# Expert scores and MLP up with one 512-wide matmul over both feature parts, and a search among 136 sums

## Chip, cores and metric

The kernel runs on one core of one Trainium2 chip. The metric is the device time of one execution in microseconds (us); each kernel is run several times and its median counts. PE is the matrix engine (TensorE), DVE is VectorE, ACT is ScalarE, POOL is GpSimd.

## What is computed

Two layers of a transformer with 256 tokens of width 1024 (a retention mixer in the first, a gated spatial unit in the second, each followed by a layer of experts), then a block with convolution and attention, attention to a memory, and an MLP with squared ReLU. All is float32. The change lies in the expert layer, and in the upward product of the MLP:

```python
def peer_ffn(h, w_query, sub_keys, expert_u, expert_v):   # 8 heads, 16 best, 128 keys
    q = (ht @ w_query).reshape(T, Hh, 2, PEER_HALF)
    scores = jnp.einsum('thpd,hpkd->thpk', q, sub_keys)
    s_top, i_top = lax.top_k(scores, K)
    cand = (s_top[:, :, 0, :, None] + s_top[:, :, 1, None, :]).reshape(T, Hh, K * K)
    best, pos = lax.top_k(cand, K)
    expert_idx = jnp.take_along_axis(cand_idx, pos, axis=-1)
    gates = jax.nn.softmax(best, axis=-1)
    a = jax.nn.gelu(jnp.einsum('tkd,td->tk', expert_u[expert_idx], x)) * gates
    return jnp.einsum('tk,tkd->td', a, expert_v[expert_idx])

def squared_relu_mlp(h, w_up, w_down):
    a = jax.nn.relu(h @ w_up)
    return (a * a) @ w_down
```

## The kernel before

**Products.** A float32 product is made of three matmuls in a reduced form of float32: features and weights are each kept as a high part and a low remainder, and high by high, high by low and low by high are added in PSUM (`mm3`, L338 to L342; `f1`, L344, for 128 outputs and 256 tokens: 8 blocks of the feature axis, 24 matmuls of 256 columns). A weight unit is 128x1024. It comes from HBM into `raw`; ACT copies out the high part (L293) and DVE, or POOL for units marked so, subtracts it to get the low part (L295). `pump` (L265) keeps three units split ahead of PE (five from the second half of layer 1's expert scores on), and it is called by `get` (L309) for each unit.

**Experts.** `peer` (L927) does not gather: it scores all 16384 experts, 128 units of 128. `u_units` makes the first 64 units (S1, called here "first half") and later the other 64 (S2): two units share a PSUM tile `pu` of 128x512, and ACT's gelu (L974) takes it to SBUF. Beside S1 runs the search for each token's experts, one small task or two at each unit (`tick`, L177): the 16 best of 128 scores for 16 key halves and two blocks of tokens (`top`, L1138 to L1145, five DVE instructions that search, find and replace), then `routing_rest` (L1147): for each of 8 heads all 256 sums (L1166), their 16 best (`pick`, again `top`), and with them the indices and gates (`prep`, `eq`, `mul`, `tree`). In S1 each fourth weight split goes to POOL. S2 runs beside the `gating` work; after it comes V, the product with the expert values (L1002 to L1106), with 512-wide matmuls.

**MLP up.** For n = 0, 2, ... 30 (L1855): two units into a `pu` tile, Relu on ACT (L1863), the square on DVE (L1865), its split by ACT (L393) and DVE (L394).

**PSUM and order.** The PSUM tiles are one bank of 512 columns each: two with the tag `mm`, two with `st`, four with `acc`. `accs` (L388) lays eight accumulators of 256 columns into the four `acc` tiles; `out_proj` (L505) uses them for the output projections of retention, the gated unit and the memory, and in the last pass a DVE operation adds each finished accumulator to the residual (`put`, L527 and L1820) while PE goes on to the next. V (L1002), the pair of query units and MLP down use `acc` tiles too. The order on each engine is written by hand: it is the order in which the code issues the instructions. A wait is set between instructions of different engines that touch the same tile.

Of the kernel before, what the change touches and what calls it, by code (L numbers as in the profile page):

```python
# [22 lines left out]
P = 128  # L23
# [134 lines left out]
class Net:  # L158
    def __init__(self, ctx, nc, tc, a, out):
        self.ctx, self.nc, self.tc, self.a, self.out = ctx, nc, tc, a, out  # L160
        self.tasks = deque()
        self.timed = {}
        self.later = deque()
        self.clock = 0

# [34 lines left out]
    def plan(self):  # L200
# [152 lines left out]

    def f1_pair(self, pss, tag, hs, shared=False, lag=0):
# [8 lines left out]
    def f2(self, pss, hs, tag, after=None, qs=range(4)):  # L363
        mm = self.nc.tensor.matmul
        for q in qs:
            s = self.get(tag)
            w = s.rearrange("p s (c m) -> p s c m", c=2)
            for tb in range(2):
                tt = slice(tb * P, tb * P + P)
                for c in range(2):  # L370
                    hi, lo = hs[2 * q + c]
# [13 lines left out]
    def acc_tile(self, name):  # L385
        return self.p_ps.tile([P, 512], F32, tag="acc", name=name, bufs=4)
# [9 lines left out]
    def split_scaled(self, his, srcs, gs):  # L396
        for (hi, lo), src, g in zip(his, srcs, gs):
            self.nc.scalar.activation(hi, src, AF.Copy, scale=g)  # L398
        for (hi, lo), src, g in zip(his, srcs, gs):
# [147 lines left out]
    def run(self):  # L547
# [9 lines left out]
        self.iota = c.tile([P, TOPK], F32, name="iota")  # L557
# [369 lines left out]
    def peer(self, l):  # L927
# [38 lines left out]
        def u_units(S, done_by, before_last=None, extra=()):  # L966
            for i in range(64):
                if i % 2 == 0:
                    pt = self.mm_tile("pu").rearrange("p (j t) -> p j t", j=2)
# [177 lines left out]
    def routing_rest(self, pr):  # L1147
        nc = self.nc
        H = 8
        sh = [P, H, TOPK, TOPK]  # L1150
        add = self.tasks.append

        def block(tb):
# [5 lines left out]
            def cand(k):  # L1159
                if k == 0:  # L1160
                    r["cand"] = pr.tile(sh, F32, tag="cand", name="cand", bufs=2)
                    r["best"] = pr.tile([P, H, TOPK], F32, tag="best", name="best")
                    r["pos"] = pr.tile([P, H, TOPK], U32, tag="pos", name="pos")
                hh = slice(4 * k, 4 * k + 4)
                s4 = [P, 4, TOPK, TOPK]
                nc.vector.tensor_tensor(r["cand"][:, hh], v4[:, hh, 0, :, None].to_broadcast(s4),  # L1166
                                        v4[:, hh, 1, None, :].to_broadcast(s4), op=ALU.add)

            def pick(h):
                self.top(pr, r["cand"][:, h].rearrange("p a b -> p (a b)"), r["best"][:, h], r["pos"][:, h], T)  # L1170

            def prep():
# [3 lines left out]
                ab = pr.tile([P, 2, H, TOPK], U32, tag="ab", name="ab")  # L1176
                nc.vector.tensor_scalar(ab[:, 0], r["pos"], 4, None, op0=ALU.logical_shift_right)
                nc.vector.tensor_scalar(ab[:, 1], r["pos"], 15, None, op0=ALU.bitwise_and)
                r["abf"] = pr.tile([P, 2, H, TOPK], F32, tag="abf", name="abf")
                nc.vector.tensor_copy(r["abf"], ab)  # L1180
# [644 lines left out]
    def mlp(self):  # L1825
# [29 lines left out]
        for n in range(0, 32, 2):  # L1855
            pt = self.mm_tile("pu").rearrange("p (j t) -> p j t", j=2)
            if n == 0:
                self.f1_pair([pt[:, 0], pt[:, 1]], "mlp_u", hs, True)
            for j in range(2 if n else 0):
                self.f1(pt[:, j], self.get("mlp_u"), hs)  # L1860
            self.tick()
            t = pa.tile([P, 2, T], F32, tag="t", name="t", bufs=2)
            nc.scalar.activation(t, pt, AF.Relu)  # L1863
# [54 lines left out]
```

## Time and profile before

| what | us |
|---|---|
| median of 3 runs | 2551.14 (2549.85 to 6877.75) |
| the profiled execution | 2548.39 |
| its span | 2546.6 |
| PE busy in it | 2483.5 |
| DVE busy | 1906.6 |
| ACT busy | 1257.2 |
| POOL busy | 212.8 |

The granted clock of PE was 0.992 of full speed over the span. The time of a run is that of the whole execution; the span is what the profiler recorded from the first instruction to the last. Busy times overlap, since the engines work beside one another. Times on a timeline are counted from the start of the span.

### The profile page before, as it was taken

Reading aid. Unit: us, or ns where it says so; the run is one execution under the profiler, and the core shown is the slowest. Engines: PE = TensorE matmul, PEld = TensorE weight load, DVE = VectorE, ACT = ScalarE, POOL = GpSimd, SP = SyncE. Lnnn points to the kernel's source line nnn. Section 1 sums busy time; section 2 is a strip of 40 time slices with the busy share of each in tenths; the row PEclk is TensorE's granted clock in tenths of the full one; section 3 lists DMA queues with packets and bytes.
Section 4 is the critical chain, followed back from the end, with each engine's and each line's share of the span. In section 5 each row is a group of like instructions: output and inputs, shape, how many; then the busy total and the mean of one; then the engine's idle time right before and its main releaser. Section 6 shows DMA issues by size and latency. Waiting matters only on the chain.

```text
span 2546.6 us, 43250 instructions
## 1 busy us (share of the span) xinstructions
PE 2483.5 (98%) x17066; PEld 2279.3 (90%) x17066; DVE 1906.6 (75%) x3230; ACT 1257.2 (49%) x1788; POOL 212.8 (8%) x155
## 2 busy tenths in 40 slices
PE   8999999999999999999999999999999999889998
PEld 7979999999988888788999999999888888889986
DVE  7767788888868777865877888888675555785654
ACT  4345544444444455556555444444445444665643
POOL 0000122200000000001122222000000000101000
PEclk8999999999999999999999999999999999999999
DMA  8785545555568888866665455555785655444553
GB/s 311 233 286 188 180 162 190 178 188 189 185 223 293 292 314 298 293 214 214 201 228 169 166 183 185 185 186 195 240 276 196 220 191 178 144 142 158 175 190 124
DMA packets 145195, 532.44 MB, mean 209 GB/s; under 512 B 16208, under 2 KB 16464, under 8 KB 144096
## 3 DMA queue, kind: packets, MB, share of 16 engines
q1 hardware_dynamic: 131616, 477.82, 56.1%
q0 software_dynamic: 12656, 49.62, 5.7%
q8 instruction: 134, 2.20, 0.4%
q10 hardware_dynamic: 720, 2.24, 0.2%
q14 instruction: 69, 0.57, 0.1%
HBM read 507.46 MB, written 22.16 MB: 208 GB/s over the span
## 4 chain that ended last, share of the span: by engine, by line
PE 74%; DVE 10%; DMA 9%; ACT 5%; issue 2%; POOL 0%; ACTq 0%; DVEq 0%; SPq 0%
PE pu L340 11%; PE pu L342 11%; PE pu L341 11%; PE V L1008 6%; PE V L1009 6%; PE V L1007 6%; DVE split L295 5%; DMA raw<-in_pv 4%; ACT split L293 3%; PE g L1275 2%; PE pq L341 1%; PE pq L342 1%; PE pq L340 1%; PE po L341 1%; PE po L342 1%
## 5 line engine op out<-in xcount | busy, mean ns | idle before, releaser
L295 DVE TENSOR_TENSOR split<-raw,split 128x1024 fp32r<-128x1024 f32 x756 | 935.6, 1241 | 515.0 <-ACT split L293 513.7
L293 ACT ACTIVATE split<-raw 128x1024 fp32r<-128x1024 f32 x808 | 851.3, 1057 | 679.2 <-PE V L1009 197.8
L340 PE MATMUL pu<-h,split 128*128 128x256 f32 x2496 | 719.8, 288 | 0.1
L342 PE MATMUL pu<-h,split 128*128 128x256 f32 x2496 | 707.1, 283 | 6.9 <-DVE split L295 6.4
L341 PE MATMUL pu<-h,split 128*128 128x256 f32 x2496 | 706.7, 283 | 0.5 <-DVE h L400 0.5
L342 PEld LDWEIGHTS pu<-h,split 128*128 128x128 f32 x2496 | 478.5, 192 | 8.4 <-DVE split L295 7.6
L341 PEld LDWEIGHTS pu<-h,split 128*128 128x128 f32 x2496 | 478.9, 192 | 0.7 <-DVE h L400 0.7
L340 PEld LDWEIGHTS pu<-h,split 128*128 128x128 f32 x2496 | 478.5, 192 | 0.6 <-ACT u L1436 0.3
L1008 PE MATMUL V<-split,a_sp 128*128 128x512 f32 x1024 | 401.9, 392 | 6.2 <-DVE split L295 6.2
L1007 PE MATMUL V<-split,a_sp 128*128 128x512 f32 x1024 | 402.3, 393 | 0.0
L1009 PE MATMUL V<-split,a_sp 128*128 128x512 f32 x1024 | 401.8, 392 | 0.0
L1008 PEld LDWEIGHTS V<-split,a_sp 128*128 128x128 f32 x1024 | 193.0, 189 | 49.5 <-DVE split L295 7.7
L1009 PEld LDWEIGHTS V<-split,a_sp 128*128 128x128 f32 x1024 | 193.0, 188 | 42.6
L1007 PEld LDWEIGHTS V<-split,a_sp 128*128 128x128 f32 x1024 | 193.1, 189 | 41.7 <-ACT split L293 0.3
L974 ACT ACTIVATE S<-pu 128x512 f32<-128x512 f32 x128 | 76.5, 598 | 232.6 <-PE pu L342 232.6
L295 POOL TENSOR_TENSOR split<-raw,split 128x1024 fp32r<-128x1024 f32 x52 | 134.0, 2576 | 527.2 <-ACT split L293 527.2
L300 DVE SCALAR_TENSOR_TENSOR raw<-raw,cact 128x1024 f32<-128x1024 f32 x92 | 111.8, 1219 | 9.3 <-DMA raw<-in_ada 5.2
L1267 DVE TENSOR_TENSOR og<-og,g 128x512 f16<-128x512 f16 x256 | 108.9, 425 | 8.8
L1285 ACT ACTIVATE stage<-g 128x256 f32<-128x256 f32 x128 | 48.8, 381 | 109.6 <-DVE S L1281 109.6
L340 PE MATMUL pq<-h,split 128*128 128x256 f32 x320 | 94.4, 295 | 1.4 <-ACT h L398 1.4
L341 PE MATMUL pq<-h,split 128*128 128x256 f32 x320 | 91.7, 287 | 0.7 <-DVE h L400 0.3
L342 PE MATMUL pq<-h,split 128*128 128x256 f32 x320 | 91.3, 285 | 0.6 <-DVE split L295 0.6
(396 smaller groups left out, 3812.2 us busy)
## 6 DMA issues: line engine op xcount, KB each, us to landing
raw<-in_pu SPq DMA_DIRECT2D x256, 512.0 KB, 3.5
raw<-in_pv SPq DMA_DIRECT2D x256, 512.0 KB, 4.5
raw<-in_ada SPq DMA_DIRECT2D x92, 512.0 KB, 4.7
raw<-in_pq SPq DMA_DIRECT2D x32, 512.0 KB, 4.1
d_g<-stage POOLq DMA_DIRECT2D x32, 512.0 KB, 3.9
g<-d_g POOLq DMA_DIRECT2D x16, 1024.0 KB, 9.8
raw<-in_mlp_u SPq DMA_DIRECT2D x32, 512.0 KB, 3.6
raw<-in_mlp_d SPq DMA_DIRECT2D x32, 512.0 KB, 3.6
```

Source lines behind the costliest of these rows:

```text
L293: nc.scalar.activation(s[:, 0], r, AF.Copy)
L295: eng.tensor_sub(s[:, 1], r, s[:, 0].bitcast(F32))
L300: nc.vector.scalar_tensor_tensor(r, r, 1.0, self.cact, op0=ALU.mult, op1=ALU.mult, accum_out=self.mod[l][:, o:o + 1])
L340: mm(ps, w_hi, x_hi, start=start, stop=False, **kw)
L341: mm(ps, w_hi, x_lo, start=False, stop=False, **kw)
L342: mm(ps, w_lo, x_hi, start=False, stop=stop, **kw)
L974: nc.scalar.activation(S[:, i - 1:i + 1], pt, AF.Gelu_apprx_tanh)
L1007: nc.tensor.matmul(o, hi, ww[:, 0], start=i == 0, stop=False)
L1008: nc.tensor.matmul(o, hi, ww[:, 1], start=False, stop=False)
L1009: nc.tensor.matmul(o, lo, ww[:, 0], start=False, stop=en)
L1267: nc.vector.tensor_tensor(og[:, k], og[:, 1], pairs(g3[:, k, tt]), op=ALU.mult)
L1275: nc.tensor.matmul(g[:, t], o1[:, t // 2, :, t % 2], og[:, k, t // 2, :, t % 2], start=k == 0, stop=k == 1)
```

## The change

Four things change. (1) In S1 of both layers and in MLP up from n = 2 on, a unit is made by `f1_wide`: for each block of features one 512-wide matmul of the high weights over the high and the low features, which lie side by side, and one 256-wide matmul of the low weights over the high features into the first half. The two halves are added by `join`, an ACT copy of the second half to SBUF and a DVE addition, and gelu or Relu then reads SBUF. (2) These units need two banks each pair, so the four `acc` tiles of one bank become two of two banks (`acc_pair`); `acc_tile` now hands out halves of such a tile to all former users. (3) In S1 each third split goes to POOL, 21 a layer instead of 16. (4) The 16 best are sought among 136 sums instead of 256, which are laid out in another way, so that `prep` computes the two positions with more steps; these and the table that they are compared with are now bfloat16.

```diff
-            us = [("w", a["pu"][P * l + i], "pu", i < 64 and i % 4 == 3) for i in range(P)]
+            us = [("w", a["pu"][P * l + i], "pu", i < 64 and i % 3 == 2) for i in range(P)]
...
+    def f1_wide(self, ps, s, hs):
+
+        mm = self.nc.tensor.matmul
+        w = s.rearrange("p s (c m) -> p s c m", m=P)
+        for c in range(KC):
+            mm(ps.rearrange("p (k t) -> p k t", k=2), w[:, 0, c], hs[c][2], start=c == 0, stop=c == KC - 1,
+               skip_group_check=True)
+            mm(ps[:, :T], w[:, 1, c], hs[c][0], start=False, stop=c == KC - 1, skip_group_check=True)
+
+    def join(self, out, pt):
+        self.nc.scalar.activation(out, pt[:, :, T:], AF.Copy)
+        self.nc.vector.tensor_tensor(out, pt[:, :, :T], out, op=ALU.add)
...
     def acc_tile(self, name):
-        return self.p_ps.tile([P, 512], F32, tag="acc", name=name, bufs=4)
+        if self.acc_half is None:
+            t = self.acc_pair(name)
+            self.acc_half = t[:, 1]
+            return t[:, 0]
+        t, self.acc_half = self.acc_half, None
+        return t
+
+    def acc_pair(self, name):
+        assert self.acc_half is None
+        return self.p_ps.tile([P, 2, 512], F32, tag="acc", name=name, bufs=2)
...
-            out += [(h[:, 0, j], h[:, 1, j]) for j in range(2)]
+            out += [(h[:, 0, j], h[:, 1, j], h[:, :, j]) for j in range(2)]
...
-        self.iota = c.tile([P, TOPK], F32, name="iota")
+        self.iota = c.tile([P, TOPK], BF16, name="iota")
...
-                self.f1(pt[:, i % 2], self.get("pu"), hs, half=self.task if i in extra else None)
+                if wide:
+                    self.f1_wide(pt[:, i % 2], self.get("pu"), hs)
+                else:
+                    self.f1(pt[:, i % 2], self.get("pu"), hs, half=self.task if i in extra else None)
...
-                if i % 2 == 1:
+                if i % 2 == 1 and wide:
+                    s = S[:, i - 1:i + 1]
+                    self.join(s, pt)
+                    nc.scalar.activation(s, s, AF.Gelu_apprx_tanh)
+                elif i % 2 == 1:
                     nc.scalar.activation(S[:, i - 1:i + 1], pt, AF.Gelu_apprx_tanh)
...
+        h8 = TOPK // 2
+        nw = TOPK + h8 * (TOPK - 1)
...
-                s4 = [P, 4, TOPK, TOPK]
-                nc.vector.tensor_tensor(r["cand"][:, hh], v4[:, hh, 0, :, None].to_broadcast(s4),
-                                        v4[:, hh, 1, None, :].to_broadcast(s4), op=ALU.add)
+                s4 = [P, 4, TOPK - 1, h8]
+                nc.vector.tensor_tensor(r["cand"][:, hh, TOPK:].rearrange("p h (a b) -> p h a b", b=h8),
+                                        v4[:, hh, 0, 1:, None].to_broadcast(s4),
+                                        v4[:, hh, 1, None, :h8].to_broadcast(s4), op=ALU.add)
...
-                self.top(pr, r["cand"][:, h].rearrange("p a b -> p (a b)"), r["best"][:, h], r["pos"][:, h], T)
+                self.top(pr, r["cand"][:, h], r["best"][:, h], r["pos"][:, h], nw)
...
-            t = pa.tile([P, 2, T], F32, tag="t", name="t", bufs=2)
-            nc.scalar.activation(t, pt, AF.Relu)
+            else:
+                pt = self.acc_pair("pu")
+                for j in range(2):
+                    self.f1_wide(pt[:, j], self.get("mlp_u"), hs)
+                self.tick()
+                self.join(t, pt)
+                nc.scalar.activation(t, t, AF.Relu)
```

ACT in S1, before: `split` is a weight unit's high part, `S` the scores; each row names what it waits for.

```order
L974 ACTIVATE S_2653<-pu 128x512 [waits PE_49]
L293 ACTIVATE split_4431<-raw_4332 128x1024 [waits DMAHW5_49,Pool_49]
L293 ACTIVATE split_4462<-raw_4364 128x1024 [waits DMAHW6_49,DVE_49,PE_49]
L974 ACTIVATE S_2653<-pu 128x512 [waits PE_49]
L293 ACTIVATE split_4494<-raw_4394 128x1024 [waits DMAHW7_49,DVE_49]
L293 ACTIVATE split_4524<-raw_4429 128x1024 [waits DMAHW0_49,DVE_49,PE_49]
```

The same stretch of ACT after the change; L365 is the copy of `join`, L1003 the gelu.

```order
L365 ACTIVATE S_2644<-pu 128x512 [waits PE_49]
L1003 ACTIVATE S_2644<-S_2644 128x512 [waits DVE_49]
L294 ACTIVATE split_3758<-raw_3667 128x1024 [waits DMAHW5_49,Activation_49]
L294 ACTIVATE split_3784<-raw_3698 128x1024 [waits DMAHW6_49,PE_49,Activation_49]
L365 ACTIVATE S_2644<-pu 128x512 [waits PE_49]
L1003 ACTIVATE S_2644<-S_2644 128x512 [waits DVE_49]
L294 ACTIVATE split_3810<-raw_3725 128x1024 [waits DMAHW7_49,Pool_49]
```

The gelu no longer waits for PE but for DVE's addition, and the two copies of weights that follow stand behind it.

DVE in MLP up, before: two weight splits, the square `r` and its split `ab`.

```order
L295 TENSOR_TENSOR split_25095<-raw_24992,split_25095 128x1024 [waits DMAHW5_49,PE_49,Activation_49]
L295 TENSOR_TENSOR split_25124<-raw_25028,split_25124 128x1024 [waits DMAHW6_49,Activation_49]
L1865 TENSOR_TENSOR r<-t 128x512 [waits Activation_49]
L394 TENSOR_TENSOR ab<-r,ab 128x512 [waits Activation_49]
L295 TENSOR_TENSOR split_25160<-raw_25057,split_25160 128x1024 [waits DMAHW7_49,PE_49,Activation_49]
```

The same after the change, with the addition of `join` (L366).

```order
L296 TENSOR_TENSOR split_24004<-raw_23921,split_24004 128x1024 [waits DMAHW3_49,Activation_49]
L296 TENSOR_TENSOR split_24025<-raw_23951,split_24025 128x1024 [waits DMAHW4_49,Activation_49]
L366 TENSOR_TENSOR t<-pu,t 128x512 [waits Activation_49]
L1914 TENSOR_TENSOR r<-t 128x512 [waits Activation_49]
L417 TENSOR_TENSOR ab<-r,ab 128x512 [waits Activation_49]
L296 TENSOR_TENSOR split_24055<-raw_23972,split_24055 128x1024 [waits DMAHW5_49,Activation_49]
L296 TENSOR_TENSOR split_24076<-raw_24002,split_24076 128x1024 [waits DMAHW6_49,Activation_49]
```

The addition stands behind both splits of weights and ahead of the square; it waits for ACT's copy.

PE in the last pass of retention's output projection (`po`), before: the end of the accumulator n = 0 and the start of n = 1.

```order
L340 MATMUL po<-ys,split_2111 128x256
L341 MATMUL po<-ys,split_2111 128x256
L342 MATMUL po<-ys,split_2111 128x256
L340 MATMUL po<-ys,split_2141 128x256
L341 MATMUL po<-ys,split_2141 128x256
```

The same place after the change.

```order
L341 MATMUL po<-ys,split_2104 128x256
L342 MATMUL po<-ys,split_2104 128x256
L343 MATMUL po<-ys,split_2104 128x256
L341 MATMUL po<-ys,split_2134 128x256 [waits DVE_49]
L342 MATMUL po<-ys,split_2134 128x256
```

The first product of n = 1 now waits for DVE, for the put of n = 0, which reads the other half of the same tile.

## Rows read from the trace of the kernel before

**Rows 1.** The page, part 4: the chain of work that ended last, by engine.

```profile
PE 74%; DVE 10%; DMA 9%; ACT 5%; issue 2%; POOL 0%; ACTq 0%; DVEq 0%; SPq 0%
```

**Rows 2.** Busy time by stretch: S1 of layer 0, a stretch of V, MLP up.

```profile
core 0: us, PE busy (x) PEld busy (x) DVE busy (x) ACT busy (x) POOL busy (x), PEclk, DMA share, GB/s
323.00:512.90 189.90, 186.69 (x1555) 186.26 (x1554) 161.66 (x392) 91.06 (x107) 42.73 (x16) 1.00 0.53 178
810.00:860.00 50.00, 50.00 (x221) 41.23 (x220) 39.93 (x48) 23.63 (x27) 0.00 (x0) 1.00 0.83 276
2361.00:2455.00 94.00, 94.00 (x764) 92.69 (x764) 62.79 (x68) 54.75 (x74) 0.00 (x0) 1.00 0.55 181
```

**Rows 3.** The waits of PE in S1 of layer 0: total, times, longest.

```profile
PE pu L342 <- DVE split L295: 3.2, 2, 1.6
```

**Rows 4.** Timeline of PE in S1: start us, duration, line, shape.

```profile
402.06 0.28 PE L341 MATMUL pu<-h,split 128*128 128x256 f32 x1
402.18 0.28 PE L342 MATMUL pu<-h,split 128*128 128x256 f32 x1
```

**Rows 5.** Timeline of PE near the end of V, layer 0.

```profile
1091.70 0.39 PE L1009 MATMUL V<-split,a_sp 128*128 128x512 f32 x1
...
1093.09 0.39 PE L1009 MATMUL V<-split,a_sp 128*128 128x512 f32 x1
```

**Rows 6.** All weight splits (second half): ns shortest, median, longest.

```profile
L295 DVE TENSOR_TENSOR split<-raw,split x756: 1159/1225/3390, 13.8 to 2525.7; 128x1024 fp32r<-128x1024 f32 x189
...
L295 POOL TENSOR_TENSOR split<-raw,split x52: 2382/2403/3397, 279.2 to 1576.5; 128x1024 fp32r<-128x1024 f32 x52
```

**Rows 7.** Timeline of DVE: starts of tops of 128 and of 256.

```profile
343.17 0.28 DVE L1140 MAX8 val<-s 128x8 f32<-128x128 f32 x1
...
344.74 0.28 DVE L1140 MAX8 val<-s 128x8 f32<-128x128 f32 x1
...
401.65 0.42 DVE L1140 MAX8 best<-cand 128x8 f32<-128x256 f32 x1
...
403.90 0.41 DVE L1140 MAX8 best<-cand 128x8 f32<-128x256 f32 x1
```

**Rows 8.** Timeline of DVE and of POOL at 339.8 us.

```profile
339.93 3.32 DVE L295 TENSOR_TENSOR split<-raw,split 128x1024 fp32r<-128x1024 f32 x1
...
339.78 2.38 POOL L295 TENSOR_TENSOR split<-raw,split 128x1024 fp32r<-128x1024 f32 x1 [10.02 <-ACT split L293]
```

**Rows 9.** Groups of MLP up, and of a retention add that reads PSUM.

```profile
L293 ACT ACTIVATE split<-raw 128x1024 fp32r<-128x1024 f32 x34 | 34.1, 1048 | 1.6 <-issue 1.6
...
L1865 DVE TENSOR_TENSOR r<-t 128x512 f32<-128x512 f32 x16 | 11.0, 689 | 15.4 <-ACT t L1863 15.4
L393 ACT ACTIVATE ab<-r 128x512 fp32r<-128x512 f32 x16 | 10.1, 632 | 13.0 <-DVE r L1865 13.0
L1863 ACT ACTIVATE t<-pu 128x512 f32<-128x512 f32 x16 | 9.5, 596 | 16.2 <-PE pu L342 15.5 <-issue 0.7
...
L1360 DVE TENSOR_TENSOR v<-pv,bv 128x512 f32<-128x512 f32 x12 | 7.7, 682 | 0.0
```

**Rows 10.** Timeline of PE and DVE, last pass of retention's output projection.

```profile
238.26 0.28 PE L340 MATMUL po<-ys,split 128*128 128x256 f32 x1
...
238.91 0.48 DVE L527 SCALAR_TENSOR_TENSOR x<-po,mod,x 128x256 f32<-128x256 f32 x1
```

**Rows 11.** Timeline of PE and DVE, last pass of the gated unit's output projection.

```profile
1311.86 0.28 PE L340 MATMUL po<-z,split 128*128 128x256 f32 x1
...
1313.65 0.48 DVE L527 SCALAR_TENSOR_TENSOR x<-po,mod,x 128x256 f32<-128x256 f32 x1
```

**Rows 12.** Timeline of PE and ACT at the end of V, layer 1.

```profile
2155.62 0.40 PE L1007 MATMUL V<-split,a_sp 128*128 128x512 f32 x1
...
2156.90 0.58 ACT L1093 ACTIVATE S<-V 128x512 f32<-128x512 f32 x1
```

**Rows 13.** Timeline of DVE and PE at the end of the kernel.

```profile
2537.22 0.75 DVE L1880 SCALAR_TENSOR_TENSOR xt<-pd,r,xt 128x512 f32<-128x512 f32 x1 [10.28 <-PE pd L375]
...
2538.19 0.40 PE L375 MATMUL pd<-split,ab 128*128 128x512 f32 x1
```

More of the change, by code (lines that the diff above doesn't have):

```diff
@@ L164, in __init__ @@
         self.clock = 0
+        self.acc_half = None
     def pool(self, name, bufs=1, **kw):
@@ L396, in split_scaled @@
     def split_scaled(self, his, srcs, gs):
-        for (hi, lo), src, g in zip(his, srcs, gs):
-            self.nc.scalar.activation(hi, src, AF.Copy, scale=g)
-        for (hi, lo), src, g in zip(his, srcs, gs):
+        for h, src, g in zip(his, srcs, gs):
+            self.nc.scalar.activation(h[0], src, AF.Copy, scale=g)
+        for (hi, lo, *_), src, g in zip(his, srcs, gs):
             self.nc.vector.scalar_tensor_tensor(lo, src, g, hi.bitcast(F32), op0=ALU.mult, op1=ALU.subtract)
@@ L966, in u_units @@
         def u_units(S, done_by, before_last=None, extra=()):
+            wide = before_last is None
             for i in range(64):
                 if i % 2 == 0:
[L969 to L970 removed]
+                    pt = self.acc_pair("pu") if wide else self.mm_tile("pu").rearrange("p (j t) -> p j t", j=2)
+                if wide:
+                    self.f1_wide(pt[:, i % 2], self.get("pu"), hs)
+                else:
+                    self.f1(pt[:, i % 2], self.get("pu"), hs, half=self.task if i in extra else None)
                 if i == 63 and before_last:
                     before_last()
[L973 removed]
+                if i % 2 == 1 and wide:
[3 more added lines that the diff above has]
+                elif i % 2 == 1:
                     nc.scalar.activation(S[:, i - 1:i + 1], pt, AF.Gelu_apprx_tanh)
@@ L1175, in prep @@
                 nc.vector.tensor_tensor(top, best, best[:, :, 0:1].to_broadcast([P, H, TOPK]), op=ALU.subtract)
[L1176 to L1180, printed above, removed]
+                ab = pr.tile([P, H, TOPK], U32, tag="ab", name="ab")
+                pf = pr.tile([P, 3, H, TOPK], F32, tag="pf", name="pf")
+                r["abf"] = pr.tile([P, 2, H, TOPK], BF16, tag="abf", name="abf")
+                nc.vector.tensor_copy(pf[:, 0], r["pos"])
+                nc.vector.tensor_scalar(ab, pf[:, 0], float(h8), -float(h8), op0=ALU.max, op1=ALU.add)
+                nc.vector.tensor_scalar(ab, ab, 3, None, op0=ALU.logical_shift_right)
+                nc.vector.tensor_copy(pf[:, 1], ab)
+                nc.vector.tensor_copy(r["abf"][:, 0], pf[:, 1])
+                nc.vector.tensor_scalar(pf[:, 2], pf[:, 0], float(TOPK), -float(h8), op0=ALU.is_ge, op1=ALU.mult)
+                nc.vector.scalar_tensor_tensor(pf[:, 0], pf[:, 1], -float(h8), pf[:, 0], op0=ALU.mult, op1=ALU.add)
+                nc.vector.tensor_add(r["abf"][:, 1], pf[:, 0], pf[:, 2])
                 r["idb"] = pr.tile([P, 16, TOPK], BF16, tag="idb", name="idb")
@@ L1855, in mlp @@
         for n in range(0, 32, 2):
-            pt = self.mm_tile("pu").rearrange("p (j t) -> p j t", j=2)
+            t = pa.tile([P, 2, T], F32, tag="t", name="t", bufs=2)
             if n == 0:
+                pt = self.mm_tile("pu").rearrange("p (j t) -> p j t", j=2)
                 self.f1_pair([pt[:, 0], pt[:, 1]], "mlp_u", hs, True)
-            for j in range(2 if n else 0):
-                self.f1(pt[:, j], self.get("mlp_u"), hs)
-            self.tick()
-            t = pa.tile([P, 2, T], F32, tag="t", name="t", bufs=2)
-            nc.scalar.activation(t, pt, AF.Relu)
+                self.tick()
+                nc.scalar.activation(t, pt, AF.Relu)
+            else:
+                pt = self.acc_pair("pu")
+                for j in range(2):
+                    self.f1_wide(pt[:, j], self.get("mlp_u"), hs)
+                self.tick()
+                self.join(t, pt)
+                nc.scalar.activation(t, t, AF.Relu)
             r = pa.tile([P, 2, T], F32, tag="r", name="r", bufs=2)
```

7 lines of the change are left out of this document (5 added, 2 removed).

## Prediction

> **What bounds the kernel now.** I read the chain of work that ended last first, then the busy time by stage, the waits of the stages that change, and the timeline at the places that the edits touch. The chain is 74% PE, 10% DVE, 9% DMA and 5% ACT [rows 1]: the matmul stream sets the end, and DVE comes next. In the first half of the expert scores of layer 0 (S1) PE is busy 186.69 of 189.90 us, DVE 161.66 [rows 2]; in MLP up PE is busy all 94.00 us, DVE 62.79. PE's whole idle time in S1 is 3.2 us, two waits for weight splits that DVE makes [rows 3]. So S1 is paced by PE, with DVE some 28 us behind.
>
> A measurement of this kernel tells about 2% (51 us) from no change. The sum below is made against the profiled execution, 2548.39 us (span 2546.6), 2.75 us under the median of the runs shown, 2551.14; I leave that difference out.
>
> **The wide matmul.** 256-wide matmuls start every 0.120 us in S1 [rows 4]: 24 of them make a unit, 2.88 us, and 64 units 184.3; the other 5.6 us of S1 are the 3.2 of waits and 2.4 of score and transpose matmuls. The new unit has 8 matmuls of 512 and 8 of 256 columns. What a 512-wide one costs is seen in V, at two paces: 221 in 50 us without a gap, 0.226 each [rows 2], and 6 starts in 1.39 us, 0.232 each [rows 5]. Which holds in S1 no row of before shows. A unit is then 8×(0.226+0.120) = 2.77 at best (−0.11) and 8×(0.232+0.120) = 2.82 (−0.06) otherwise; the columns stay 6144, so a loss has no source, and nothing is the other bound. I take 2.82, since S1's 256-wide pace, twice which is 0.240, lies nearer the slower one. It is −0.06 × 158 units (64 in each layer, 30 in MLP up) = −9.5 us, if PE remains the bound.
>
> The Trainium skill, TensorE: Matmul & The Clock Gate, section "Wait — 56ns, not 53.3ns?", says that a warm matmul costs its columns at 2.4 GHz and some 2.5 ns more. By it only the 8 saved starts count, 20 ns a unit, an estimated 3.2 us in all, and the sum would be up to 6.3 us higher; the rows' 0.120 is well above the 0.109 that it gives for 256 columns, so I go by the rows.
>
> **What S1 pays for it on DVE and ACT.** Per layer, 32 joins are added. Each is an ACT copy of 128x512 from PSUM (0.60, as the Relu that reads PSUM [rows 9]) and a DVE add with one operand in PSUM (0.68 [rows 9], about 0.65 net of overlap): DVE +20.8, ACT +19. Taken from DVE: 5 more splits go to POOL (21 instead of 16), −5×1.15 (median 1.225 [rows 6], less the overlap with what follows) = −5.7. The 16 picks shrink: a top of 128 starts 1.57 after the one before, one of 256 2.25 [rows 7]; 136 wide is 1.61 in proportion, −0.64×16 = −10.2. Half as many candidates and some small operations more on the positions I set against each other, at nothing (bounds −2 and +2; DVE's slack covers it). DVE: 161.7+20.8−5.7−10.2 = 166.6 us. That is under 180.5+2.4 = 183 us of PE work, but it lies unevenly. While the tops run, at one a unit, six units need 6×1.57 + 4 splits×1.15 + 3 joins×0.65 = 16.0 us of DVE against 6×2.82 = 16.9 of PE; and a split that starts beside a POOL split takes 3.32 instead of 1.2, since POOL holds it up from 339.78 to 342.16 [rows 8]. With one such block the six units need 18.1. At the start of S1 two tops come per unit, so DVE is late there as in the waits of before.
>
> The Trainium skill, SBUF — State Buffer, section "Who interferes with whom", says that a DVE instruction with two inputs in SBUF and a GpSimd instruction that reads SBUF block each other wholly, and that one with at most one SBUF input does not. The trace agrees for the split (3.32); by the rule the add of the join, with one input in PSUM, would go free, which no row of before shows.
>
> Without any rule, the add's bounds are 0.68 and 0.68+2.38 (a whole POOL split [rows 6, 8]); I take 0.68, its form in a row. The chain from a pair's last matmul grows too: copy 0.60, add 0.68, gelu 0.60 (as the Relu), then the next weight's ACT copy 1.05 [rows 9] and, on POOL, 2.4 to 3.4 for its split [rows 6]: 5.3 to 6.3 and handshakes, where PE gives two units, 5.64. Behind the waiting gelu on ACT stand the next two weights, and PE waits for those. I put PE's idle time at 7 us a layer (5 for DVE, 2 for POOL units; bounds 0 and 13). S1: 64×2.82 = 180.5, +2.4, +7 = 189.9, that is no change; two layers: 0, bounds −13 and +12.
>
> **MLP up.** PE's pair falls from 5.76 to 5.64, but the loop through ACT and DVE is now add 0.69, Relu 0.60, product 0.69, copy 0.63, two weight copies of 1.05 less 0.05 each, since they overlap, and the second one's DVE split 1.15 [rows 6, 9], one after another in the engines' order: 5.8. DVE's next add stands behind that split. So 15 pairs × (+0.05) = +0.8 us; bounds −1.8 (PE paces) and +6 (handshakes of 0.4 a pair).
>
> **What the shared PSUM tiles add.** The four accumulators were tiles of their own; now two share a tile, and an instruction that writes one half waits for the reader of the other. The built order shows it in the last pass of three output projections: the products of n = 1, 3, 5, 7 wait for the DVE put of n−1. In retention, n = 1 began at 238.26 on PE, while that put runs from 238.91 for 0.48 [rows 10]: 1.2 us. Later a put follows its product at once: the end of the last matmul 0.28, put 0.48, about 0.75 with handshakes: 3×0.75, together 3.4. In the gated unit n = 1 began at 1311.86 and the put ends at 1314.13 [rows 11]: 2.3+2.2 = 4.5. Memory: four such steps at 0.7 (its put is a plain add, a little shorter), 2.8. All are on PE, and the weights are ready, so nothing hides them. V ends twice a layer with the same wait, there for the ACT copy: some 0.85 (copy 0.60 and two handshakes), but 1.9 where that copy ends at 2157.48 and PE went on at 2155.62 [rows 12]: 4.4. At the end the closing step of the first half waits for the last matmul, which began at 2538.19 and ends 0.40 later, instead of starting at 2537.22 [rows 13]: 1.4. Sum 3.4+4.5+2.8+4.4+1.4 = +16.5; bounds 5 (PE makes up what splits it finds ready) and 22.
>
> **Sum.** 2548.4 + 0 + 0.8 + 16.5 = 2565.7 us.
>
> **Rivals.**
> 1. Not slower: DVE keeps up with the joins, so that PE paces S1, and the 512-wide matmul runs at the faster of the two paces. Then S1 loses 0.11×64 = 7 and its idle time falls from the 3.2 of before to about 0: −10 a layer; MLP −1.8 (PE paces it too), shared tiles +16.5: 2543.1, below the time of before. With DVE keeping up but the slower pace it is −0.06×64 and −1.2 of idle time, −5 a layer: 2553.1. For it: DVE's sum is 16 us under PE's, and 0.226 is seen in long stretches of V. Against it: S1's own 256-wide pace goes with the slower one, and two waits for DVE stand there already. It decides from the point where DVE's six units with a blocked split, 18.1, meet slack of 1.2 from the units around them.
> 2. POOL's 21 splits collide with DVE's two-operand work: each blocks a split for 2.1 more on one or the other side. If half of the 21 do so where DVE has no slack, +11 a layer: 2565.7+22 = 2588. For it: the block of 3.32 [rows 8]; against it: before, 16 such splits cost PE 3.2 us only.
> 3. Slower beyond 2%: the join's chain binds every pair in S1 and MLP. Price: copy 0.60 and add 0.68 stand between a pair and its gelu; if the ring of weights no longer covers them, 79 pairs × 0.6 to 0.7 = +47 to +55 on top of the sum: about 2615. It decides from the point where a pair's chain is over 5.64 us for DVE units as well; for those I count 0.6+0.68+0.6+1.05+1.2 = 4.1 (1.05 and 1.2 being the ACT copy and the split) plus DVE's queue, so it needs 1.5 us of queue at each pair.
>
> **Chances.** Forecast 0.53 (own range 2559 to 2575), rival 1 0.27 (0.10 of it at the faster pace), rival 2 0.15, rival 3 0.05. To leave out no more than 2 in 10 the range goes from 2545 to 2588. Faster by over 2% (under 2497) would take more than all of the wide matmul's bound of 17 us: 0.01. Slower by over 2% (over 2599) is rival 3: 0.04. Within 2%: 0.95.
>
> **What would show it.** Right: 512-wide scores starting 0.23 after one another with 0.12 for the narrow ones; S1 about 190 us long with PE idle 5 to 9 on DVE and POOL splits; DVE near 167 us in it; waits of PE for the puts in the output projections, with four gaps each, and for the V copies. Wrong: S1 of 183 us or less (rival 1), of 200 or more (rival 2), or pairs of 6.3 us everywhere (rival 3); output projections without gaps would take 10 us or more off the sum.

## The result, and the profile after

The changed kernel takes 2590.7 us (median of 6 runs, 2583.46 to 2596.29), the kernel before 2549.36 in the same comparison: 1.0167 times as long, with a 95% interval of 1.0155 to 1.0179, or 41 us more. 2565.7 was predicted, with 2545 to 2588 as range. The direction was right, the size was not: the loss is two and a half times the predicted one, and the median lies 2.7 us above the range.

The chain of the changed kernel's page has PE at 72% where it had 74% [rows 1], and more of DVE:

```profile
PE 72%; DVE 12%; DMA 6%; ACT 6%; issue 3%; POOL 1%; SPq 0%; ACTq 0%; DVEq 0%
```

Where the 41 us came from is read by stage. The table gives the length of stages in the profiled executions, each from the start of one tile's first matmul on PE's timeline to that of another (spans: 2546.6 before, 2589.4 after).

| stage (PE's timeline) | before | after | difference |
|---|---|---|---|
| retention's output projection (PE's waits for the puts alone) | 0 | 3.0 | +3.0 |
| S1 and S2 of layer 0 (first `pu` to first `V`) | 412.3 | 420.5 | +8.2 |
| V of layer 0 | 361.2 | 360.1 | −1.1 |
| gated unit's output projection (first to last `po<-z`) | 72.4 | 81.7 | +9.3 |
| S1 and S2 of layer 1 | 412.3 | 421.0 | +8.7 |
| V of layer 1 | 352.9 | 355.2 | +2.3 |
| attention, memory and its output projection | 119.5 | 131.3 | +11.8 |
| MLP up | 95.5 | 95.3 | −0.2 |
| after the last `pd` matmul | 8.4 | 9.5 | +1.1 |

Two sums stand out: S1 and S2 with +17 for both layers (0 was predicted), and the places with shared tiles with +27.5 (16.5 was predicted).

**S1.** Busy time of S1 of layer 0 (the columns are those of [rows 2]):

```profile
326.20:523.40 197.20, 184.08 (x1041) 158.04 (x1040) 175.97 (x428) 106.97 (x138) 51.59 (x21) 1.00 0.51 168
```

It lasts 197.2 us where it lasted 189.9 [rows 2], with DVE busy 175.97 instead of 161.66. PE's waits in it:

```profile
PE pu L362 <- POOL split L296: 5.6, 7, 1.7
PE pu L362 <- DVE split L296: 2.9, 4, 1.2
PE ptr L1262 <- DVE ent L1257: 2.8, 2, 1.4
PE pu L360 <- ACT split L294: 1.8, 1, 1.8
```

The 3.2 us of [rows 3] have become 13.1, for splits of POOL and DVE, a weight copy of ACT, and `ent`, the end of the search, which PE transposes. One of the waits for POOL, followed back (the rows are in the order of the chain, from PE to what held it up first):

```profile
354.52 0.38 PE L362 MATMUL pu<-h,split 128*128 128x256 f32 x1 [1.57 <-POOL split L296]
352.11 2.37 POOL L296 TENSOR_TENSOR split<-raw,split 128x1024 fp32r<-128x1024 f32 x1 [9.83 <-ACT split L294]
350.99 1.99 ACT L294 ACTIVATE split<-raw 128x1024 fp32r<-128x1024 f32 x2
350.45 0.63 ACT L1003 ACTIVATE S<-S 128x512 f32<-128x512 f32 x1 [4.66 <-DVE S L366]
349.73 0.68 DVE L366 TENSOR_TENSOR S<-pu,S 128x512 f32<-128x512 f32 x1
348.61 1.21 DVE L296 TENSOR_TENSOR split<-raw,split 128x1024 fp32r<-128x1024 f32 x1
```

POOL was not slow here (2.37): it began late, because the weight's copy on ACT stood behind the gelu, the gelu behind the addition, and the addition behind a split on DVE. Nine of the fourteen waits, 8.1 of the 13.1 us, go through a gelu that waits for its addition in this way. The waits stand beside a gain, for a unit of 8 wide and 8 narrow matmuls goes from the first of these rows to the second (PE's timeline, start and duration):

```profile
449.82 0.39 PE L360 MATMUL pu<-h,split 128*128 128x512 f32 x1
...
452.59 0.39 PE L360 MATMUL pu<-h,split 128*128 128x512 f32 x1
```

That is 2.77 us, against 2.88 by [rows 4]: 0.11 less, the better of the two bounds. Not every unit runs so: of the 63 steps from unit to unit in this S1, 30 take 2.77 us, 16 take 2.79 to 2.86 and the others hold a wait; in layer 1 15 take 2.77 and 30 the slower time. Both paces of the prediction occur, and the mean over the pairs of matmuls without a gap is 0.349 us, or 2.79 a unit (layer 1: 0.351, or 2.81). In 64 units PE gains some 6 us. The gaps between its matmuls that are longer than their pace sum to 17.3 us, where they were 4.2: 13.1 more, and 13.1 less 6 is the 7.3 within 0.2. What fills DVE is seen in its groups of instructions in S1 (count, then busy us and mean ns), here of the kernel before:

```profile
L295 DVE TENSOR_TENSOR split<-raw,split 128x1024 fp32r<-128x1024 f32 x48 | 62.6, 1304 | 23.4 <-ACT split L293 23.4
L1193 DVE TENSOR_TENSOR eq<-abf,iota 128x1024 bf16<-128x1024 f32 x8 | 14.0, 1771 | 0.0
...
L1204 DVE TENSOR_TENSOR tree<-tree 128x512 bf16<-128x512 bf16 x4 | 1.7, 428 | 0.1
```

and the groups that answer to them after the change:

```profile
L296 DVE TENSOR_TENSOR split<-raw,split 128x1024 fp32r<-128x1024 f32 x43 | 61.1, 1423 | 13.0 <-ACT split L294 12.6
L366 DVE TENSOR_TENSOR S<-pu,S 128x512 f32<-128x512 f32 x31 | 21.2, 683 | 3.5 <-ACT S L365 3.1
L1237 DVE TENSOR_TENSOR eq<-abf,iota 128x1024 bf16<-128x1024 bf16 x8 | 15.3, 1915 | 0.0
...
L1248 DVE TENSOR_TENSOR tree<-tree 128x512 bf16<-128x512 bf16 x4 | 3.8, 944 | 0.1
L1213 DVE TENSOR_TENSOR top<-best 128x128 f32<-128x128 f32 x2 | 2.8, 1383 | 0.0
```

The joins (L366) are as predicted, 0.683 each. The split's mean rose from 1304 to 1423 ns, although one that nothing blocks takes 1225 [rows 6]; `eq`, now all in bfloat16, rose to 1915, a level of the tree from 428 to 944. These are instructions with two operands in SBUF, and what lengthens them is POOL's splits, as with this one on DVE and the one on POOL beside it:

```profile
425.41 3.09 DVE L296 TENSOR_TENSOR split<-raw,split 128x1024 fp32r<-128x1024 f32 x1 [0.20 <-ACT split L294]
424.50 2.91 POOL L296 TENSOR_TENSOR split<-raw,split 128x1024 fp32r<-128x1024 f32 x1 [11.96 <-ACT split L294]
```

(1423−1225) × 43 = 8.5 us on the splits alone, where it was (1304−1225) × 48 = 3.8. Over all of DVE's instructions in this S1, those that ran beside a POOL split and took longer than the shortest of their group lost 21.7 us (15 of them), where before they lost 10.8 (5 of them).

**The shared tiles.** The gated unit's output projection, PE at the end of the accumulator n = 0 and the start of n = 1:

```profile
1319.26 0.28 PE L343 MATMUL po<-z,split 128*128 128x256 f32 x1
1323.99 0.55 PE L341 MATMUL po<-z,split 128*128 128x256 f32 x1 [4.46 <-DVE x L550]
```

and what DVE and ACT do then:

```profile
1321.14 1.06 ACT L294 ACTIVATE split<-raw 128x1024 fp32r<-128x1024 f32 x1 [4.78 <-DMA raw<-in_sgu_o]
...
1322.23 1.23 DVE L296 TENSOR_TENSOR split<-raw,split 128x1024 fp32r<-128x1024 f32 x1 [6.87 <-ACT split L294]
1323.37 0.48 DVE L550 SCALAR_TENSOR_TENSOR x<-po,mod,x 128x256 f32<-128x256 f32 x1
```

PE stands 4.6 us. The put (L550) that it waits for is behind a weight's split on DVE, that behind the weight's copy on ACT, and that waits for its DMA. Then comes what the prediction had no word of. PE's granted clock (the column ahead of the DMA share) before, after and well after that wait:

```profile
1316.00:1319.30 3.30, 3.30 (x31) 3.30 (x29) 0.00 (x0) 0.36 (x1) 2.39 (x1) 1.00 0.96 356
1324.00:1326.00 2.00, 2.00 (x9) 2.00 (x10) 0.99 (x1) 1.68 (x3) 0.00 (x0) 0.50 1.02 416
1330.00:1332.00 2.00, 2.00 (x19) 2.00 (x19) 1.74 (x3) 1.71 (x4) 0.00 (x0) 0.99 0.00 0
```

It falls from 1.00 to 0.50, that is from 2.4 to 1.2 GHz; the 256-wide matmuls start 0.213 us apart instead of 0.117, until about 1330: some 28 of them, 2.7 us. The other three waits are 0.82 each (0.94 between starts), near the 0.75 predicted, and leave the clock at 1.00. In the memory's output projection both happen again. PE's waits for the puts there (total, times, longest):

```profile
PE po L341 <- DVE x L1864: 7.1, 4, 4.0
```

The latest of these puts on DVE's timeline stands behind a split and seven instructions for the next features and their norm, and began without a pause behind them:

```profile
2390.07 0.41 DVE L1864 TENSOR_TENSOR x<-po,x 128x256 f32<-128x256 f32 x1
```

Before the change the same puts stood as late, behind the same work, and nothing waited for them:

```profile
2350.02 0.42 DVE L1820 TENSOR_TENSOR x<-po,x 128x256 f32<-128x256 f32 x1
...
2355.49 0.42 DVE L1820 TENSOR_TENSOR x<-po,x 128x256 f32<-128x256 f32 x1
```

The products that now wait for these two began at 2348.30 and 2351.31 on PE. The clock in three stretches after the change, the first ahead of the waits:

```profile
2350.00:2360.00 10.00, 8.69 (x57) 7.64 (x56) 5.58 (x10) 6.54 (x12) 0.00 (x0) 1.00 0.17 54
2386.00:2393.00 7.00, 2.95 (x14) 2.66 (x13) 4.57 (x10) 4.26 (x12) 0.00 (x0) 0.50 0.23 75
2393.00:2398.00 5.00, 4.49 (x22) 4.19 (x20) 2.75 (x8) 2.15 (x7) 0.60 (x1) 0.50 0.06 15
```

From start to start the four waits lost 7.9 us (2.2, 0.7, 4.3 and 0.7), and 31 matmuls that start 0.214 us apart instead of 0.118 another 3.0: together nearly all of the 11.8. At the end of V the two waits of layer 0 come out at 0.85 (1.08 between starts, less 0.233), and those of layer 1 at 1.9 and 0.85, all as predicted, but after the longer one nine matmuls start 0.38 to 0.43 us apart, once more half of the clock.

### The profile page after: what moved, and what is told of

The parts are those of the page before. It is cut to its first block, busy times and chain, and to the rows that moved or that the text cites. A ratio compares the mean times of both kernels' runs of the same rounds, so it can differ in the third digit from the quotient of the medians.

```text
span 2589.4 us, 40899 instructions
## 1 busy us (share of the span) xinstructions
PE 2490.4 (96%) x15802; PEld 2219.4 (86%) x15802; DVE 1948.7 (75%) x3323; ACT 1298.3 (50%) x1867; POOL 230.6 (9%) x165
## 4 chain that ended last, share of the span: by engine, by line
PE 72%; DVE 12%; DMA 6%; ACT 6%; issue 3%; POOL 1%; SPq 0%; ACTq 0%; DVEq 0%
PE V L1038 7%; PE V L1039 7%; PE V L1040 7%; PE pu L360 7%; PE pu L341 5%; PE pu L343 5%; PE pu L342 5%; DVE split L296 5%; PE pu L362 4%; ACT split L294 3%; DMA raw<-in_pv 2%; PE g L1319 2%; PE po L341 2%; PE po L342 2%; PE po L343 2%
## 5 line engine op out<-in xcount | busy, mean ns | idle before, releaser
L360 PE MATMUL pu<-h,split 128*128 128x512 f32 x1264 | 448.0, 398 | 3.8 <-ACT split L294 3.6
L362 PE MATMUL pu<-h,split 128*128 128x256 f32 x1264 | 357.5, 283 | 15.0 <-POOL split L296 9.0
L341 PE MATMUL pu<-h,split 128*128 128x256 f32 x1232 | 360.7, 293 | 0.1
L343 PE MATMUL pu<-h,split 128*128 128x256 f32 x1232 | 349.0, 283 | 0.5 <-DVE split L296 0.2
L342 PE MATMUL pu<-h,split 128*128 128x256 f32 x1232 | 348.9, 283 | 0.0
L360 PEld LDWEIGHTS pu<-h,split 128*128 128x128 f32 x1264 | 238.0, 188 | 59.1 <-ACT split L294 4.4
L362 PEld LDWEIGHTS pu<-h,split 128*128 128x128 f32 x1264 | 239.4, 189 | 22.6 <-POOL split L296 13.6
L343 PEld LDWEIGHTS pu<-h,split 128*128 128x128 f32 x1232 | 236.4, 192 | 1.1 <-POOL split L296 0.7
L342 PEld LDWEIGHTS pu<-h,split 128*128 128x128 f32 x1232 | 236.9, 192 | 0.0
L341 PEld LDWEIGHTS pu<-h,split 128*128 128x128 f32 x1232 | 236.5, 192 | 0.4 <-ACT u L1480 0.3
L296 POOL TENSOR_TENSOR split<-raw,split 128x1024 fp32r<-128x1024 f32 x62 | 151.7, 2446 | 529.5 <-ACT split L294 529.5
```

The costliest lines, as they stand in the source:

```text
L296: eng.tensor_sub(s[:, 1], r, s[:, 0].bitcast(F32))
L341: mm(ps, w_hi, x_hi, start=start, stop=False, **kw)
L342: mm(ps, w_hi, x_lo, start=False, stop=False, **kw)
L343: mm(ps, w_lo, x_hi, start=False, stop=stop, **kw)
L360: mm(ps.rearrange("p (k t) -> p k t", k=2), w[:, 0, c], hs[c][2], start=c == 0, stop=c == KC - 1, skip_group_check=True)
L362: mm(ps[:, :T], w[:, 1, c], hs[c][0], start=False, stop=c == KC - 1, skip_group_check=True)
```

## Experiments

Each was compared with the kernel before on the same chip; times are medians, ratios against before with their 95% intervals.

**Alternating halves.** Neighbouring accumulators lie in different tiles.

```diff
         t = [self.acc_tile(name) for _ in range(4)]
+        t = [t[0], t[2], t[1], t[3]]
         return [t[n % 4][:, (n // 4) * T:(n // 4) * T + T] for n in range(KC)]
...
+        V = [[V[tb][half] for tb in range(2)] for half in range(2)]
```

> The changed kernel, but neighbouring accumulators lie in different shared tiles (n = 0, 2, 4, 6 in one, 1, 3, 5, 7 in the other), and V's two token blocks too. Theory: the shared tiles cost 25 of the 41 us (retention's output projection 3, the gated unit's 9.5, the memory's 12), since a product waits for a put that stands late on DVE. With one product of 2.8 us more between them, 14 to 20 us come back: 2571 to 2577. Rival: these puts are late for other reasons (a late weight transfer), and PE would wait there anyway: 2586 to 2594, as now.

2571.29 us, 1.0079 (1.0057 to 1.0100), 19 less than the changed kernel. Retention's waits are gone, the gated unit's stage is 74.9 us long instead of 81.7, V of layer 1 351.4 instead of 355.2; the memory's keeps most of its loss (127.6 against 119.5), because its four products of a unit take 0.7 us each, too short to cover a late put. PE's waits for puts there:

```profile
PE po L341 <- DVE x L1866: 5.1, 2, 3.8
```

So it is the sharing that makes PE wait, and the order of the halves is most of the price.

**The tiles alone.** The kernel before with `acc_tile` and `acc_pair` of the changed one and nothing else.

```diff
     def acc_tile(self, name):
-        return self.p_ps.tile([P, 512], F32, tag="acc", name=name, bufs=4)
+        if self.acc_half is None:
+            t = self.acc_pair(name)
...
+        return self.p_ps.tile([P, 2, 512], F32, tag="acc", name=name, bufs=2)
```

> The kernel before, with nothing but the two-bank tiles whose halves are handed out. Theory: 25 us more than before, 2574 (2568 to 2580), with the waits of PE for the puts as in the changed kernel and S1 at 190 us. Rival, the prediction's sizes: 16.5 more, 2566. Rival that blames S1 and MLP alone: 2549.

2580.62 us, 1.0116 (1.0094 to 1.0138), just above the theory's range: 31 more than before by the medians, 26 by the spans of the profiles (2572.8 against 2546.6). S1 and S2 are 412.3 us in both layers, as before; the gated unit's stage is +9.6, the memory's +9.8, V of layer 1 +2.1, and PE's waits are near those of the changed kernel. In retention:

```profile
PE po L341 <- DVE x L537: 3.0, 4, 1.0
```

In the gated unit:

```profile
PE po L341 <- DVE x L537: 6.7, 4, 4.7
```

The larger part of the 41 us is thus no matter of the matmul at all.

**Each fourth split on POOL,** as before the change.

```diff
-            us = [("w", a["pu"][P * l + i], "pu", i < 64 and i % 3 == 2) for i in range(P)]
+            us = [("w", a["pu"][P * l + i], "pu", i < 64 and i % 4 == 3) for i in range(P)]
```

> The changed kernel with each fourth split of S1 on POOL (16) as before, not each third (21). Theory that POOL's longer splits and the port they share with DVE make S1 late: S1 192 us instead of 197, 2581. Rival that DVE's sum of work makes it late: DVE gets 5 splits of 1.2 more a layer, S1 200 us or more, 2596.

2601.92 us, 1.0201 (1.0178 to 1.0223): 11 more, so the rival's direction. S1 and S2 last 426.3 us in both layers, 5.9 and 5.3 more for five splits on DVE. PE waits for no POOL split any longer, but for DVE's:

```profile
PE pu L362 <- DVE split L296: 7.6, 8, 3.6
```

**S1 narrow,** all else as changed.

```diff
-            wide = before_last is None
+            wide = False
```

> The changed kernel with S1's units as before (24 matmuls of 256, gelu from PSUM, no join); MLP up stays wide, 136 sums, each third split on POOL and the shared tiles stay. Theory: the joins are what S1 pays, so S1 goes back to 187 to 190 us: 2591 less 15, 2576. Rival that POOL's third split is to blame: S1 stays at 195 or more, 2588.

2565.99 us, 1.0060 (1.0040 to 1.0080). S1 and S2 last 408.6 and 408.5 us, 12 a layer less than changed and 3.7 less than before. The joins cost 12 us net a layer, and what the shorter search and POOL's part give is 3.7.

**Each second split on POOL** (`i % 2 == 1` in the line above, 32 a layer).

> The changed kernel with each second split of S1 on POOL (32 a layer). Theory that DVE's sum of work sets S1's pace: 11 splits fewer on DVE, about 1.16 each by the run with 16, take 8 to 12 us from S1 until PE is the bound at about 185: the two layers 16 to 24 less, 2567 to 2575. Rival, blocks between POOL and DVE on the shared port eat what DVE gives up: 2585 to 2600.

2602.46 us, 1.0206 (1.0189 to 1.0223): the rival holds, 2.5 above its range (the profile is of an execution of 2616.91). With POOL busy for 77 us of S1, `eq` takes 2447 ns and the product `mul`, too, is blocked (DVE's groups, mean ns):

```profile
L296 DVE TENSOR_TENSOR split<-raw,split 128x1024 fp32r<-128x1024 f32 x33 | 42.0, 1275 | 14.4 <-ACT split L294 13.7
...
L1237 DVE TENSOR_TENSOR eq<-abf,iota 128x1024 bf16<-128x1024 bf16 x8 | 19.6, 2447 | 0.0
L1242 DVE TENSOR_TENSOR eq<-eq,idb 128x2048 bf16<-128x2048 bf16 x4 | 9.3, 2318 | 0.0
```

Of the three shares tried a third is the best. DVE is not full here (171.5 us busy up to S1's end and the start of S2); beside the blocks it waits 14.3 us for the ACT copies ahead of its additions. Which of the two weighs more stays open.

**No addition.** The join's DVE instruction is left out in S1, and with it half of each product.

```diff
-                    self.join(s, pt)
+                    self.nc.scalar.activation(s, pt[:, :, T:], AF.Copy)
```

> The changed kernel without the DVE addition of the join in S1 (gelu reads the copied half alone; the other half of each product is left out). Theory that DVE's work sets the pace: 32 x 0.68 = 22 us of DVE go, S1 falls from 197 to about 184, PE's own time, as far as in the run with narrow S1 or below: 2565. Rival that the longer chain through ACT (copy, then gelu) makes the weights late: S1 stays at 192 or more, 2581 or more.

2570.07 us, 1.0084 (1.0067 to 1.0101), and S1 ends after 186.3 us instead of 197.2, though the copy on ACT is still made (busy time by stretch):

```profile
326.70:513.00 186.30, 179.79 (x1037) 157.45 (x1037) 156.63 (x397) 110.20 (x138) 52.40 (x21) 1.00 0.54 179
```

So 11 of the 12 us that the joins cost are the addition's. It takes two things away at once, though: 21 us of DVE's work, and the wait of the gelu for DVE. The next run takes away the second alone. PE is still not full (179.79).

**Gelu one unit later.** On ACT a weight's copy now stands ahead of the gelu that waits for DVE.

```diff
-                    nc.scalar.activation(s, s, AF.Gelu_apprx_tanh)
+                    self.timed.setdefault(self.clock + 1, []).append(
+                        lambda s=s: nc.scalar.activation(s, s, AF.Gelu_apprx_tanh))
```

> The changed kernel with S1's gelu issued one unit later, so that on ACT a weight's copy stands ahead of the gelu that waits for DVE's addition. Theory that DVE's sum of work sets the pace: nothing changes, 2587 to 2594. Rival that the chain copy, addition, gelu, weight copy, split is what PE waits for: S1 189 us or less, 2575 or less.

2578.45 us, 1.0119 (1.0096 to 1.0142): 12 less, between the two expectations. Layer for layer S1 and S2 fall by 4 and 6 us (416.5 and 415.0), the rest of the difference lies in V of layer 0 (358.0 against 360.1) and elsewhere, where nothing was edited. PE's waits in S1 of layer 0 fall from fourteen to six, 8.8 us, and none goes through a gelu any longer; what is left is splits and `ent`, late on DVE and POOL. So the gelu that waits for DVE did keep back the weights on ACT, for 4 to 6 us a layer, and the rest of the loss does not need it.

**The search and POOL's part alone:** the kernel before with the 136 sums and each third split on POOL.

```diff
-            us = [("w", a["pu"][P * l + i], "pu", i < 64 and i % 4 == 3) for i in range(P)]
+            us = [("w", a["pu"][P * l + i], "pu", i < 64 and i % 3 == 2) for i in range(P)]
...
-        self.iota = c.tile([P, TOPK], F32, name="iota")
+        self.iota = c.tile([P, TOPK], BF16, name="iota")
...
-                self.top(pr, r["cand"][:, h].rearrange("p a b -> p (a b)"), r["best"][:, h], r["pos"][:, h], T)
+                self.top(pr, r["cand"][:, h], r["best"][:, h], r["pos"][:, h], nw)
```

> The kernel before with the 136 sums and each third split on POOL; no wide matmul, no shared tiles, no join. Theory: DVE is relieved by some 16 us a layer, PE's waits of 3.2 go, S1 186 us: 2549 less 7, 2542. Rival that more POOL splits cost as much as the shorter search gives: 2549 to 2552.

2536.47 us, 0.9956 (0.9942 to 0.9971): faster than both kernels; of the 12 us under the one before, 7.5 lie in S1 and S2 (408.5 and 408.6). PE has no wait left in S1, and DVE 41 us of room (busy time by stretch):

```profile
322.20:508.50 186.30, 186.30 (x1557) 186.30 (x1556) 144.98 (x399) 91.06 (x108) 53.71 (x21) 1.00 0.56 181
```

**The 136 sums alone,** with each fourth split on POOL.

> The kernel before with the 136 sums alone (each fourth split on POOL as before). Theory: DVE is relieved by 10 us a layer, all after the tops, where PE did not wait; the two waits for splits at the start of S1 stay, so nothing moves: 2546 to 2551. Rival: the shorter search is what made the run with both parts 12 us faster: 2535 to 2541.

2543.87 us, 0.9982 (0.9973 to 0.9991), between the two expectations. S1 and S2 last 412.3 us in both layers, to the tenth as before, and the two waits of [rows 3] are there:

```profile
PE pu L342 <- DVE split L295: 3.2, 2, 1.6
```

So the 3.8 us a layer of the run above need the splits on POOL; whether these would do it without the shorter search was not tried. That this kernel is a fifth of a per cent faster all the same comes from stages that it doesn't touch (V of layer 0 is 358.6 instead of 361.2). In that stage PE's pace is the same in both kernels, 0.229 us a matmul; the gaps beyond it sum to 7.2 us instead of 9.6. Why these gaps come and go from run to run I leave open.

**Every second pair wide,** with joins of 256 columns from one-bank tiles, gelu late, accumulators as before, MLP up narrow, 136 sums, each third split on POOL.

```diff
-            wide = before_last is None
+            first = before_last is None
             for i in range(64):
...
+                wide = first and i // 2 % 2 == 1
...
+                    pt = self.acc_tile("pu")
+                    self.f1_wide(pt, self.get("pu"), hs)
+                    self.join(S[:, i], pt)
```

> 136 sums and each third split on POOL, accumulators in tiles of their own as before, MLP up narrow; in S1 every second pair of units is wide, each unit in a one-bank tile with a join of 256 columns, gelu one unit late. Theory: DVE has room for half of the joins (145 + 13 + some 5 of blocks = 163 of 184 us), so PE is the bound and gains 32 x 0.106 = 3.4 us a layer: 2531 (2528 to 2535). Rival: joins make single splits late wherever they stand: 2540 or more.

2543.41 us, 0.9983 (0.9974 to 0.9992): 7 more than without any wide unit. The rival holds: S1 and S2 last 413.1 and 411.6 us, where without wide units they last 408.5, and PE waits 4.4 in S1, for one split and for `ent`, though DVE is busy only 160 of 185.5 us there. DVE's sum leaves room; single instructions are late nevertheless.

**Alternating halves and late gelu together,** in the changed kernel.

> The changed kernel with alternating accumulators and gelu one unit late, both together. Theory of two separate causes: the gains of the two runs add up, 20 + 12: 2559 (2554 to 2564). Rival of one common cause: no better than the better one, 2568 to 2573.

2562.72 us, 1.0055 (1.0039 to 1.0070): 28 less than changed, where 19.4 and 12.3 add up to 31.7. The causes are separate for the most part.

**All units wide, tiles as before:** the run with every second pair wide, with all of them (`wide = first`).

> As the run with every second pair wide, but all units of S1 wide. Theory that DVE's sum sets the pace: 145 + 27 of joins + 10 of blocks = 182 us of some 184, S1 at 190 to 193: 2549 to 2556, level with the kernel before, since no tile is shared. Rival that sharing tiles is the whole loss: as fast as PE allows, 180 a layer: 2525.

2551.38 us, 1.0012 (1.0002 to 1.0021). With accumulators in tiles of their own the wide S1, the late gelu, the shorter search and POOL's third together are level with the kernel before. By stage it is not a balance in S1: S1 and S2 last 418.3 and 414.0 us, 15 more for both layers than with the last two alone, and V of both layers is 8.9 shorter than before, though nothing was edited there. S1 of layer 0 is as long as the theory said (192 us), but DVE is busy for 170 of them and not 182 of 184, so a full DVE is not the reason; PE waits 9.2 us, for splits and for `ent`.

## Why the prediction was wrong, point by point

**The wide matmul** (predicted 2.82 us a unit): 2.79 and 2.81 on the mean of the two layers. This was right; the units run at 2.77 or at 2.82, so neither bound holds alone. What sets a unit's pace was not found.

**S1** (predicted: no change). The step that failed is PE's idle time, put at 7 us a layer: it was 13.1 by the waits (17.3 from start to start), partly paid by the faster unit, which leaves +7.3 in S1. Two terms under it were too small. The first is DVE's sum, 166.6 us, which was 175.97: its parts came out (joins 0.683, picks −10.2, splits; the small operations set at nothing came to about +1), but it held POOL's blocks at their size of before, and they grew from 10.8 to 21.7. The second is the chain of the gelu. The prediction names it, with an addition of 0.68, but prices no wait of the addition in DVE's queue; nine of PE's fourteen waits went that way, and the run with the late gelu got 4 to 6 us a layer back.

The blocks are the second rival's mechanism, which had 11 a layer. That they cost PE time is seen row by row in one place: a small operation ahead of `ent` took 1.86 us beside a POOL split (0.17 elsewhere), and PE stood 1.4 for that `ent`. How much of the other waits is theirs, and how much is the mere order on DVE, no run here separates: the run with a fourth of the splits on POOL (5.3 to 5.9 a layer more for five splits) speaks for DVE's work, the one with half of them for the blocks, and the one with every second pair wide shows single splits late with 25 us of DVE's time left.

By the Trainium skill (SBUF — State Buffer, "Who interferes with whom") an addition with one operand in PSUM does not contend with POOL. The trace agrees: in S1 of both layers no join was held up, though 12 of them ran beside a POOL split, so the upper bound of 0.68+2.38 was never met (shortest, median and longest of 64, in ns):

```profile
L366 DVE TENSOR_TENSOR S<-pu,S x64: 671/682/694, 333.1 to 1612.0; 128x512 f32<-128x512 f32 x64
```

Not every instruction with one operand in SBUF goes free, as the prediction has it: the small operation above (`den`, in place, 1.86 instead of 0.17) was held up, and so was a cast (`g`, 1.39 instead of 0.23; before, 2.30).

**MLP up** (predicted +0.8): −0.2, near in time by luck, since the term was wrong. The additions of the joins follow one another at 6.0 us in the steady part, so the loop through ACT and DVE is longer than the 5.8 worked out; but PE runs ahead of it, and from the first wide matmul at 2402.44 to the first of MLP down it waits 0.2 us in all:

```profile
PE pu L360 <- DVE t L366: 0.2, 1, 0.2
```

So PE paced the stage. Its fifteen pairs take 5.87 us each, where they took 5.91 before; where only these matmuls run, a pair takes 5.65 to 5.69 after and 5.67 to 5.80 before. Only the last two pairs (6.0 each) are held by the loop. The wide matmul gains next to nothing here, and the first pair, still narrow, began at half of the clock behind the memory's waits.

**The shared tiles** (predicted +16.5): +27.5 in the changed kernel, and 21.5 in the three stages of the run with the tiles alone, to which retention's waits of 3.0 and the end come. Retention (3.4, measured 3.0 by the waits and 3.7 from start to start), V's waits (4.4, measured 0.85+0.85+1.9+0.85) and the end (1.4, measured 1.1) were right. Three steps failed. In the gated unit I took a row at 1311.86 for the start of n = 1, which lay near its end: counted back from the last matmul of the pass, n = 1 begins at 1309.35, so that the wait is 4.8 and not 2.3 (measured 4.6). In the memory's projection I priced four puts as if DVE were free for them; they stand behind a split and behind the features' seven instructions, 2.2 and 4.3 us for two of them, and the trace of before has these puts at 2350.02 and 2355.49, where it could have been read. And for all of them I priced the wait alone: after the long ones PE went on at half of its clock.

**The end of the range,** 2588, was the second rival's sum with the shared tiles at 16.5. With these at their measured size that rival gives 2599.

## What to carry to other kernels

Two accumulators in one PSUM tile are one object to the waits: before tiles are merged to make room for a wider operation, each former user has to be walked through, also those far from the edit, for what stands ahead of the reader on its engine. Where DVE has 28 us of room beside PE in a stage of 190, as here, a join of 0.68 us for each 5.5 us of matmul was too dear; the sum of DVE has to be taken with POOL's blocks, and room in the sum did not keep single splits from being late: an instruction that hands work from one engine to the next has to be priced with the queue that it stands in. The part of an edit that was thought of as company, the shorter search with a third of the splits on POOL, ran 12 us faster alone, 7.5 of them in the stages that it touches.

## What was not expected of the hardware

In three places PE's granted clock was 0.50 after a wait for a shared tile: after 4.6 us of standing in the gated unit, from the first long wait of the memory's projection on (2.2 us), and after 1.9 at the end of V in layer 1. 256-wide matmuls then started 0.213 us apart instead of 0.117, 512-wide ones 0.43 instead of 0.233, for 3 us and more. In the gated unit this added 2.7 us to a wait of 4.6. The kernel before shows it too, behind other waits: 0.50 from 761 to 767 us, after 4.0 us between two starts in V of layer 0. In S1 of layer 1 after the change, two gaps in a row, of 2.10 and 1.26 us from start to start, took the clock to 0.50 at 1507.5. Single gaps of 1.6 to 2.1 us in S1 of layer 0 left it at 1.00, and so did one of 2.31 in the memory's projection of the run with the tiles alone, the same gap that is followed by 0.50 in the changed kernel. So the length of one gap is not all that counts; what else does was not tried. The Trainium skill (TensorE: Matmul & The Clock Gate, "HAM oscillation — how this bites in real kernels") tells of waits for DMA between groups of matmuls after which the next group starts throttled; the rows here agree, with waits for DVE and ACT.

The bfloat16 table did not make `eq` faster: the median of its 128x1024 form is 1215 ns over 16 in the changed kernel and 1220 before.
